# The stages before layer 0's scores, rearranged: adaLN loads, context tiles, weight products, PSUM pairs

## The chip, the cores and the metric

The kernel runs on one core of one Trainium2 chip. The metric is the device time of one execution in microseconds (us). The core has five engines that run beside each other and wait for one another through semaphores: TensorE (PE in the profile; its weight loads are PEld), VectorE (DVE), ScalarE (ACT), GpSimd (POOL) and SyncE (SP), which here issues most of the DMA transfers.

## What is computed

Two layers of a diffusion backbone over 1024 latent tokens and 256 context tokens, width 1024. Layer 0 mixes tokens by multi-head latent attention (16 heads), layer 1 by differential attention (8 heads). Cut to what matters for this change, which lies in layer 0:

```python
shift, scale, gate = split(silu(c) @ ada_w + ada_b, 3)           # latent; shift_c, scale_c, gate_c from c_ctx
h, h_c = x * (1 + scale) + shift, ctx * (1 + scale_c) + shift_c
q_lat, kv_lat, k_pe, g = split(h @ w_in, [256, 384, 416])        # the same for h_c
q = rms_norm(q_lat, g_qa) @ w_qb        # 16 heads of 64 + 32 (rotary)
k, v = split(rms_norm(kv_lat, g_kva) @ w_kvb)                    # 16 heads of 64 and 64; k_pe shared
o = softmax(q @ concat(k, k_c) * scale) @ concat(v, v_c)         # context queries see the context alone
x = layer_norm(ALPHA * x + gate * ((o * silu(g)) @ out_w)) 
```

## The kernel before, in words

The kernel keeps fp32 accuracy by splitting operands into a high part and a remainder (`split`, L175: ScalarE copies the high part, VectorE or GpSimd subtracts it) and multiplying three times (`mm3`, L184). Contraction over the width is in 8 blocks of 128 (`KT`); tokens are in 10 tiles of 128, of which 8 and 9 are context.

**Order of the work.** The program is written as straight Python; a scheduler orders the instructions of each engine and inserts the waits. Inside a `manual_schedule` block the engines named there (TensorE from L205 on, TensorE and VectorE in L880) keep the order in which the program is written; the other engines get theirs from the scheduler. SP issues its transfers in one in-order queue.

**adaLN (L196 to L251).** Per block `k` two 512 KB blocks of `ada_w` are loaded into six shared buffers (one of which holds a bias row first): for `g = 1` (the scale) TensorE multiplies the block by the broadcast SiLU of the conditioning (L228), for `g = 0` (the shift) VectorE accumulates it into `acc[0]` (latent) and `acc[1]` (context) (L232). From `k = 2` on, `in_weight(k - 2)` follows (L214): it loads 128 rows of the input weight's first 416 columns (208 KB) into a staging buffer `xt` (14 of them) and splits it into `wAH`, `wAL`; GpSimd subtracts for k = 6 and 7, VectorE otherwise. `shift_cols(s)` (L238) sums `acc[s]` over partitions on TensorE (L241) and copies the result to `cols0` (L243).

**Modulation and the latent projections (L254 to L385).** `h_part` loads a block of transposed tokens into an `xt` buffer and makes its modulated high part on ScalarE (L260) and its remainder on VectorE (L261, L263; for every third block GpSimd does L263). First all eight blocks of the context (both its tiles at once), then a few warm-up matmuls (L269), then `lat_mm` of tile 8 for blocks 0 to 3, then `shift_cols(0)`, then the first 512 latent tokens, then the rest of tile 8. The loop from L357 takes the other tiles in the order 9, 0 to 7, each with its eight blocks in one go; RMS statistics, normalisation, and turning (`lat_post`) follow three tiles behind.

**Gates and up-projection weights (L311 to L610).** TensorE works through 40 gate tiles (4 column groups of 10 token tiles). Beside them `up_weights` loads the Q and K weights: each block is multiplied by its norm gain on VectorE (L397 for Q, 768 columns; L307 for K and V, 512 columns) and split; squares of the weights (L407 to L410, ScalarE) are summed by TensorE (L418) to bound the values. Then `ada_dve` accumulates three more adaLN thirds on VectorE; the first product of each is L509, the others L511. `v_weight` loads the V weights.

**K, Q and V (L613 to L883).** PSUM has 8 banks of 512 columns. `set_banks` gives three pairs (tag `a`) and two single banks (`d`). A fixed list (L881) interleaves the generators: `pq`, `pk` project Q and K of head 0 and split them with a scale (`split16`), `vg` makes one V tile (L642 to L657), and `pm` makes the row of maxima for head 0: one step for each of four query tiles (L757, L759), one for the context's keys (L763 to L765), one that turns the row by TensorE (L768) and writes it into the Q operand (L769). For an even V tile ScalarE makes two copies and GpSimd the remainder (L650, L653, L654); for an odd one ScalarE makes one and VectorE the remainder (L650, L656).

**Heads (L905 to L957).** `run_step` takes units of scores, exponentials (L777), their casts (L778) and remainders (L779), with side work between. In head 0 the side work holds `ab1_of` and `h1_range` (L537 to L565): small VectorE instructions with one TensorE step (L552) that bound layer 1's input. They stand ahead of that head's `max0` in the program.

Of the kernel before, what the change touches and what calls it, by code (L numbers as in the profile page):

```python
# [53 lines left out]
def hybrid_kernel(  # L54
# [159 lines left out]
    def in_weight(k):  # L214
        ws = hs.tile([P, 512], F32, tag="xt", bufs=14, name=nm("ws"))
        sp.dma_start(ws[:, :NA], w_in[k * P:(k + 1) * P, :NA])
        split(wAH[:, k, :], wAL[:, k, :], ws[:, :NA], e_lo=pool if k > 5 else None)

    for k in range(KT):
        for g in (1, 0):  # L220
            w = hs.tile([P, D], F32, tag="adaw", bufs=6, name=nm("adaw"))
            sp.dma_start(w, ada_w[0, k * P:(k + 1) * P, g * D:(g + 1) * D])
            if k == 0 and g == 0:
                for s in range(2):
                    sp.dma_start(acc[s][0:1, :], ada_b[0:1, :D])
            if g:
                for j in range(KT):
                    pe.matmul(cbs[j // 4][:, j % 4, :], w[:, j * P:(j + 1) * P], scb[:, k, :], start=False,  # L228
                              stop=(k == KT - 1), skip_group_check=True)
            else:  # L230
                for s in (1, 0):
                    dve.scalar_tensor_tensor(acc[s], w, sc[:, 2 * k + s:2 * k + s + 1], acc[s], op0=ALU.mult, op1=ALU.add)  # L232
        if k > 1:
            in_weight(k - 2)
    for i in range(2):
        dve.tensor_scalar_add(cols0[:, 8 + 4 * i:12 + 4 * i, :], cbs[i][:, :, 0:2], 1.0)

    def shift_cols(s):  # L238
        cb = bank("d")
# [8 lines left out]
            mm3(ps[:, :NA], hH[:, k, ts], hL[:, k, ts], wAH[:, k, :], wAL[:, k, :], k == 0, k == KT - 1)  # L248

    shift_cols(1)  # L250
    for k in (6, 7):  # L251
        in_weight(k)

    def h_part(pool_, bufs, c0, n, k):  # L254

# [7 lines left out]
        (pool if k % 3 == 2 else dve).tensor_tensor(hL[:, k, c0:c0 + n], xt[:, :n], fv(hi), op=ALU.subtract)  # L263

    for k in range(KT):
        h_part(hs, 14, *CHUNKS[2], k)
    ps8 = bank("a")
    for _ in range(4):
        pe.matmul(ps8[:, :NA], idr, wAH[:, 0, :], start=True, stop=True)  # L269
    lat_mm(ps8, 8, range(4))  # L270
    shift_cols(0)
    for k in range(KT):
        h_part(hs, 14, *CHUNKS[0], k)
    lat_mm(ps8, 8, range(4, KT))
    hs_ctx.close()
    upw = rp.enter_context(spool("upw", side="right"))
    wqH = upw.tile([P, 2, 1536], F32R, name="wqH")
# [26 lines left out]

    def kv_weight(c, hi, lo, ws, e_lo=pool):
        sp.dma_start(ws, w_kv[:, c])
        dve.tensor_scalar_mul(ws, ws, gkva)  # L307
        split(hi, lo, ws, e_lo=e_lo)


# [30 lines left out]
    with spool("p0a") as pa:  # L341
# [15 lines left out]
        for t in (8, 9, 0, 1, 2, 3, 4, 5, 6, 7, None, None, None):  # L357
# [3 lines left out]
            if t is None:  # L361
# [1 line left out]
                    pass  # L363
                gate_tile(0, *wg)
                continue
            ps = ps8
            if t != 8:
                ps = bank("a" if t % 2 == 0 else "b")
                lat_mm(ps, t, range(KT))
            with tc.high_priority():  # L370
# [16 lines left out]
    def up_weights(pa):  # L387
# [5 lines left out]
        def q_weight(j, hh):  # L393
            c = slice(hh * 768, hh * 768 + 768)
            ws = u()
            sp.dma_start(ws, w_qb[j * P:(j + 1) * P, c])
            dve.tensor_scalar_mul(ws, ws, gqa[:, j:j + 1])  # L397
            split(wqH[:, j, c], wqL[:, j, c], ws)

        def k_weight(hh):  # L400
# [78 lines left out]
    def ada_dve(tile_, thirds):  # L479
# [25 lines left out]
        def add(k, s):  # L505
            ck = sc[:, 2 * k + s:2 * k + s + 1]
            if k == 0:
                acc.append(tile_("acc"))
                dve.tensor_scalar_mul(acc[s], ws[k], ck)  # L509
            else:  # L510
                dve.scalar_tensor_tensor(acc[s], ws[k], ck, acc[s], op0=ALU.mult, op1=ALU.add)  # L511

# [97 lines left out]
            pass  # L610
    p0.close()

    set_banks(a=3, d=2)  # L613
    a0 = ctx.enter_context(ExitStack())
    wk = a0.enter_context(spool("a0work"))
    Vh = wk.tile([P, NT, H0, V0 + 1], F16, name="Vh")
# [23 lines left out]
    def prod_v0():  # L640
        pool.memset(Vh[:, :, :, V0:V0 + 1], 1.0)
        for t in range(NT):  # L642
            ts = slice(t * P, (t + 1) * P)
            ps = pair()
            for hh in range(2):
                c = slice(hh * 512, hh * 512 + 512)
                mm3(ps[:, c], latH[:, 2, ts], latL[:, 2, ts], wv[0][:, c], wv[1][:, c], True, True)
            src = ps.rearrange("p (h d) -> p h d", d=V0)
            vh = Vh[:, t, :, :V0]
            act.activation(vh, src, AF.Copy, scale=vsc0)  # L650
            if t % 2 == 0:
                vf = w0("op").rearrange("p a b -> p (a b)")[:, :1024].rearrange("p (h d) -> p h d", d=V0)
                act.activation(vf, src, AF.Copy, scale=vsc0)  # L653
                pool.tensor_tensor(Vl[:, t, :, :], vf, vh, op=ALU.subtract)  # L654
            else:
                dve.scalar_tensor_tensor(Vl[:, t, :, :], src, vsc0, vh, op0=ALU.mult, op1=ALU.subtract)  # L656
            yield  # L657
# [221 lines left out]
    pm = max0(0, 0)  # L879
    with tc.manual_schedule(engines={ET.PE, ET.DVE}):  # L880
        for g in (pq, pk, pq, vg, pq, pq, vg, pk, pk, pq, pq1, vg, pq2, pq2, pq2, vg,  # L881
                  pm, vg, pm, vg, pm, vg, pm, vg, pm, vg, pm, vg):
            next(g)  # L883
    ow_ctx = ExitStack()

    def first(g, n):
# [18 lines left out]
    for h in range(H0):  # L905
# [42 lines left out]
        else:  # L948
            kq = chain(prod_k(h + 1), prod_q(h + 1, 0))
            low = [[(first(lw, 3), p_)] if h == H0 - 2 else [] for p_ in ((1, 0, 1, 0, 1), (1, 0, 1, 0, 1))]  # L950
            if h == 0:
                ab1_of()
            hr = [(h1_range(pair), (0, 1, 0, 1, 1))] if h == 0 else []
            run_step(units0(h, 0), hr + [(max0(h, 1), (1, 1, 2, 1, 1)), (max0(h, 2), (0, 1, 0, 1)),
                                    (kq, (2, 2, 1 + quad, 0, 0) if even else (2,))] + low[0])
            qs = chain(prod_q(h + 1, 1), prod_q(h + 1, 2))
# [719 lines left out]
```

## Time and profile before

| | us |
|---|---|
| median of 3 runs (lowest, highest) | 1806.28 (1804.34, 1807.49) |
| the profiled execution's own time | 1809.26 |
| its span, first to last instruction | 1807.5 |
| TensorE busy | 1671.3 |
| VectorE busy | 1241.4 |
| ScalarE busy | 1119.5 |
| GpSimd busy | 796.1 |
| mean granted TensorE clock (1 is full speed) | 0.986 |

The profile is one execution, and times in it count from its first instruction. A group's row gives line, engine, operation, output<-inputs and count, then busy time, the mean of one in ns, and the idle time ahead with what ended it. A wait's row gives who waited for whom, the total, the times and the longest. A row of the timeline gives start, duration, and in brackets the idle time before it. A row of the table of stretches gives each engine's busy time, the granted clock and the DMA engines' busy share and rate.

### The profile page before, as it was taken

Reading aid. Unit: us, or ns where it says so; the run is one execution under the profiler, and the core shown is the slowest. Engines: PE = TensorE matmul, PEld = TensorE weight load, DVE = VectorE, ACT = ScalarE, POOL = GpSimd, SP = SyncE. Lnnn points to the kernel's source line nnn. Section 1 sums busy time; section 2 is a strip of 40 time slices with the busy share of each in tenths; the row PEclk is TensorE's granted clock in tenths of the full one; section 3 lists DMA queues with packets and bytes.
Section 4 is the critical chain, followed back from the end, with each engine's and each line's share of the span. In section 5 each row is a group of like instructions: output and inputs, shape, how many; then the busy total and the mean of one; then the engine's idle time right before and its main releaser. Section 6 shows DMA issues by size and latency. Waiting matters only on the chain. (4 is left out here: it accounts for less than half of the span.)

```text
span 1807.5 us, 36761 instructions
## 1 busy us (share of the span) xinstructions
PE 1671.3 (92%) x14564; PEld 1236.1 (68%) x14564; DVE 1241.4 (69%) x2047; ACT 1119.5 (62%) x2233; POOL 796.1 (44%) x722
## 2 busy tenths in 40 slices
PE   7999979999999998999999999989999999986998
PEld 6999955656666665577766666767676757574776
DVE  7558575565665657547745777777877787969564
ACT  3541167777777787845535676767676766766442
POOL 1522146767776676835541222232314132435454
PEclk9999999999999999999999999999999999998999
DMA  8258510111111113164432213131212121223332
GB/s 303 80 157 263 160 46 22 42 45 25 37 44 36 46 39 103 33 212 160 144 108 59 80 54 78 54 80 54 68 41 58 40 66 55 67 61 121 97 120 70
DMA packets 111225, 154.84 MB, mean 86 GB/s; under 512 B 13415, under 2 KB 84679, under 8 KB 111054
## 3 DMA queue, kind: packets, MB, share of 16 engines
q1 hardware_dynamic: 102654, 144.90, 27.1%
q10 hardware_dynamic: 8400, 7.61, 1.3%
q8 instruction: 114, 1.87, 0.5%
q14 instruction: 57, 0.47, 0.1%
HBM read 98.65 MB, written 27.07 MB: 70 GB/s over the span
## 5 line engine op out<-in xcount | busy, mean ns | idle before, releaser
L779 POOL TENSOR_TENSOR pl<-p,ph 128x1024 f16<-128x1024 f32 (+1 forms) x176 | 366.1, 2085 | 153.6 <-ACT ph L778 127.0
L1358 ACT ACTIVATE p<-ps_b,mx 128x512 f32<-128x512 f32 (+1 forms) x384 | 230.7, 618 | 89.3 <-DVE mx L1354 85.2
L777 ACT ACTIVATE p<-ps_a,esc 128x1024 f32<-128x1024 f32 (+1 forms) x176 | 189.2, 1075 | 98.1 <-PE ps_a L835 92.1
L759 DVE TENSOR_REDUCE mx<-ps_a 128x1 f32<-128x1024 f32 x128 | 155.3, 1222 | 130.6 <-PE ps_a L757 130.6
L778 ACT CAST ph<-p 128x1024 f16<-128x1024 f32 (+1 forms) x176 | 177.1, 1006 | 5.5
L1352 DVE TENSOR_REDUCE mx<-ps_b 128x1 f32<-128x512 f32 x256 | 165.7, 682 | 0.0
L848 PE MATMUL ps_d<-Vh,pl 128*128 128x65 f16 x1344 | 147.1, 194 | 3.1 <-POOL pl L779 3.1
L845 PE MATMUL ps_d<-Vh,ph 128*128 128x65 f16 x1344 | 149.2, 196 | 0.0
L847 PE MATMUL ps_d<-Vl,ph 128*128 128x64 f16 x1344 | 148.0, 193 | 0.0
L1335 PE MATMUL ps_b<-KS,QS 128*128 128x512 f16 (+1 forms) x384 | 125.8, 345 | 13.8 <-DVE pl L182 7.2
L1383 POOL TENSOR_TENSOR sm<-sm,us 128x1 f32<-128x1 f32 x64 | 16.8, 262 | 273.3 <-DVE sm L1362 268.5
L845 PEld LDWEIGHTS <-ph 128*128 128x128 f16 x1344 | 123.9, 98 | 18.1 <-issue 5.0
L847 PEld LDWEIGHTS <-ph 128*128 128x128 f16 x1344 | 124.6, 99 | 12.4 <-issue 0.6
L833 PE MATMUL ps_a<-qH,KH 100*128 100x512 f16 x320 | 122.7, 383 | 10.0 <-ACT p L777 5.1
L1336 PE MATMUL ps_b<-KS,Q 128*128 128x512 f16 (+1 forms) x384 | 128.9, 345 | 0.0
L181 ACT ACTIVATE ph<-ps_b,lcf 128x512 f16<-128x512 f32 (+1 forms) x192 | 115.4, 649 | 19.1 <-PE ps_b L1371 19.1
L848 PEld LDWEIGHTS <-pl 128*128 128x128 f16 x1344 | 123.8, 98 | 4.3 <-POOL pl L779 4.2
L182 DVE SCALAR_TENSOR_TENSOR pl<-ps_b,lcf,ph 128x512 f16<-128x512 f32 (+1 forms) x192 | 117.2, 655 | 13.4 <-ACT ph L181 13.4
L1371 PE MATMUL ps_b<-idr,p 128*128 128x128 f32 x640 | 103.4, 278 | 22.7 <-ACT p L1358 14.8
L834 PE MATMUL ps_a<-qH,KL 96*128 96x512 f16 x320 | 122.5, 383 | 0.0
L835 PE MATMUL ps_a<-qL,KH 96*128 96x512 f16 x320 | 121.5, 380 | 0.0
L1381 PE MATMUL ps_b<-vh,pl 128*128 128x128 f16 x640 | 111.3, 220 | 5.3 <-DVE pl L182 5.3
(427 smaller groups left out, 5261.2 us busy)
## 6 DMA issues: line engine op xcount, KB each, us to landing
ws<-in_dw SPq DMA_DIRECT2D x28, 512.0 KB, 3.9
adw<-in_ada_w SPq DMA_DIRECT2D x24, 512.0 KB, 4.8
adaw<-in_ada_w SPq DMA_DIRECT2D x16, 512.0 KB, 7.5
g<-sg_d SPq DMA_DIRECT2D x16, 512.0 KB, 4.0
sg_d<-gg ACTq DMA_DIRECT2D x40, 128.0 KB, 3.4
o_d<-op SPq DMA_DIRECT2D x7, 640.0 KB, 3.9
xt<-in_xT SPq DMA_DIRECT2D x16, 256.0 KB, 4.4
wgs<-in_w_in SPq DMA_DIRECT2D x32, 128.0 KB, 2.7
```

The source lines that it names most:

```text
L759: dve.tensor_reduce(mx[:, t, 0:1], ps, axis=AX.X, op=ALU.max)
L777: act.activation(p32[:, :n], st, AF.Exp, scale=esc0)
L778: act.copy(ph[:, :n], p32[:, :n])
L779: pool.tensor_tensor(pl[:, :n], p32[:, :n], ph[:, :n], op=ALU.subtract)
L833: pe.matmul(s_, kh[:nr, ks], QH[:nr, :], start=True, stop=False)
L845: pe.matmul(pv[:, t, :], ph[:, ts], Vh[:, k, h, :], start=(k == kcs[0] and t == 0), stop=False, skip_group_check=True)
L847: pe.matmul(pv[:, t, :V0], ph[:, ts], Vl[:, k, h, :], start=False, stop=False, skip_group_check=True)
L848: pe.matmul(pv[:, t, :], pl[:, ts], Vh[:, k, h, :], start=False, stop=(k == NT - 1), skip_group_check=True)
L1335: pe.matmul(out, qs[m][:, ts], ks[m][:, c0:c0 + n], start=True, stop=False)
L1336: pe.matmul(out, q1[m][:, ts], ks[m][:, c0:c0 + n], start=False, stop=True)
L1352: dve.tensor_reduce(mx[:, 2 + 2 * m + i:3 + 2 * m + i], b, axis=AX.X, op=ALU.max, negate=True)
L1358: act.activation(p[m][:, c0:c0 + n], b, AF.Exp, bias=nb, accum_out=sm[:, 2 + 3 * m + i:3 + 3 * m + i])
```

## The change

In the order of the program:

- The input weights' blocks no longer stand among the adaLN blocks: `in_weight(k)` is called just before the context's `h_part` of the same block. GpSimd subtracts for every odd k. The last adaLN pair comes in the order shift, scale. The copies of the scale (L236) come after `shift_cols(1)`.
- Both context tiles have a PSUM bank from the start and are accumulated block by block, tile 8 and tile 9 in turn; `shift_cols(0)` comes after block 3 of both; the first 512 latent tokens come after all of it.
- The multiplications by norm gains (L307, L397) and the first product of each adaLN third (L509) go from VectorE to ScalarE.
- K, Q and V have four PSUM pairs and no single bank; the three pairs and two banks come back after the list. Odd V tiles now have their remainder from GpSimd, even ones from VectorE. In the list the context's maxima come ahead of V tiles 7 and 8, and the turned row ahead of the last.
- `ab1_of` and `h1_range` go from head 0 to head 2.

```diff
     def in_weight(k):
...
-        split(wAH[:, k, :], wAL[:, k, :], ws[:, :NA], e_lo=pool if k > 5 else None)
+        split(wAH[:, k, :], wAL[:, k, :], ws[:, :NA], e_lo=pool if k % 2 else None)
 
     for k in range(KT):
-        for g in (1, 0):
+        for g in (1, 0) if k < KT - 1 else (0, 1):
...
-        if k > 1:
-            in_weight(k - 2)
-    for i in range(2):
-        dve.tensor_scalar_add(cols0[:, 8 + 4 * i:12 + 4 * i, :], cbs[i][:, :, 0:2], 1.0)
...
     shift_cols(1)
-    for k in (6, 7):
-        in_weight(k)
+    for i in range(2):
+        dve.tensor_scalar_add(cols0[:, 8 + 4 * i:12 + 4 * i, :], cbs[i][:, :, 0:2], 1.0)
...
     for k in range(KT):
+        in_weight(k)
         h_part(hs, 14, *CHUNKS[2], k)
-    ps8 = bank("a")
+    psc = {8: bank("a"), 9: bank("b")}
     for _ in range(4):
-        pe.matmul(ps8[:, :NA], idr, wAH[:, 0, :], start=True, stop=True)
-    lat_mm(ps8, 8, range(4))
-    shift_cols(0)
+        pe.matmul(psc[8][:, :NA], idr, wAH[:, 0, :], start=True, stop=True)
+    for k in range(KT):
+        for t in (8, 9):
+            lat_mm(psc[t], t, (k,))
+        if k == 3:
+            shift_cols(0)
     for k in range(KT):
         h_part(hs, 14, *CHUNKS[0], k)
-    lat_mm(ps8, 8, range(4, KT))
...
     def kv_weight(c, hi, lo, ws, e_lo=pool):
-        dve.tensor_scalar_mul(ws, ws, gkva)
+        act.activation(ws, ws, AF.Copy, scale=gkva)
...
-            ps = ps8
-            if t != 8:
+            if t > 7:
+                ps = psc[t]
+            else:
...
-            dve.tensor_scalar_mul(ws, ws, gqa[:, j:j + 1])
+            act.activation(ws, ws, AF.Copy, scale=gqa[:, j:j + 1])
...
-                dve.tensor_scalar_mul(acc[s], ws[k], ck)
+                act.activation(acc[s], ws[k], AF.Copy, scale=ck)
...
-    set_banks(a=3, d=2)
+    set_banks(a=4)
...
-            if t % 2 == 0:
+            if t % 2:
...
         for g in (pq, pk, pq, vg, pq, pq, vg, pk, pk, pq, pq1, vg, pq2, pq2, pq2, vg,
-                  pm, vg, pm, vg, pm, vg, pm, vg, pm, vg, pm, vg):
+                  pm, vg, pm, vg, pm, vg, pm, pm, vg, vg, pm, vg):
             next(g)
+    set_banks(a=3, d=2)
...
-            if h == 0:
+            if h == 2:
                 ab1_of()
-            hr = [(h1_range(pair), (0, 1, 0, 1, 1))] if h == 0 else []
+            hr = [(h1_range(pair), (0, 1, 0, 1, 1))] if h == 2 else []
```

## The prediction

> **What bounds the kernel now.** I read the page first, for the shares, then the table of stretches, since the change touches only what comes before layer 0's scores (to 256 us) and one step in each of heads 0 and 2.
>
> ```profile
> span 1807.5 us, 36761 instructions
> PE 1671.3 (92%) x14564; PEld 1236.1 (68%) x14564; DVE 1241.4 (69%) x2047; ACT 1119.5 (62%) x2233; POOL 796.1 (44%) x722
> ```
> ```profile
> core 0: us, PE busy (x) PEld busy (x) DVE busy (x) ACT busy (x) POOL busy (x), PEclk, DMA share, GB/s
> 4.00:31.00 27.00, 20.71 (x143) 19.54 (x144) 20.39 (x21) 2.79 (x6) 0.76 (x1) 1.00 1.01 381
> 42.00:108.00 66.00, 66.00 (x428) 64.84 (x426) 38.06 (x70) 36.76 (x112) 28.31 (x40) 1.00 0.42 122
> 108.00:118.00 10.00, 7.61 (x57) 6.74 (x55) 8.26 (x17) 4.18 (x9) 0.00 (x0) 1.00 0.41 117
> 118.00:221.00 103.00, 102.97 (x828) 98.91 (x828) 73.36 (x93) 22.87 (x56) 21.91 (x24) 1.00 0.66 195
> 221.00:256.00 35.00, 27.52 (x119) 19.64 (x118) 23.24 (x22) 21.27 (x24) 12.21 (x7) 0.96 0.31 81
> 251.00:257.00 6.00, 3.90 (x11) 2.32 (x12) 2.66 (x4) 3.14 (x3) 2.06 (x1) 0.72 0.00 0
> 273.00:278.00 5.00, 5.00 (x38) 2.75 (x36) 1.23 (x1) 2.16 (x2) 1.60 (x2) 0.66 0.01 3
> ```
>
> TensorE is busy 92% of the span, and where it is full (42 to 108, 118 to 221) no other engine's saving shows: there only what TensorE itself starts earlier counts, and it counts whole, because everything behind follows TensorE. The rest divides in four: the adaLN stage, where the DMA engines are full (share 1.01, 381 GB/s) and TensorE waits; 2.4 us of waits in 108 to 118; 7.5 us of waits in 221 to 256 (K, Q, V), with the granted clock at 0.72 at their end; and head 0, where the clock is again at 0.66. The four terms of the sum are these four places.
>
> **Term 1: adaLN first, context block by block.** First the transfer rate, then steps in order of time, then the weight loads' group (count, busy, mean ns).
>
> ```profile
> 16.00:28.00 12.00, 7.55 (x62) 6.88 (x60) 10.18 (x12) 1.76 (x4) 0.00 (x0) 1.00 1.02 397
> ```
> ```profile
> 19.69 0.42 SPq L216 DMA_DIRECT2D ws<-in_w_in  x1
> 21.05 2.14 SPq L222 DMA_DIRECT2D adaw<-in_ada_w  x2
> ...
> 30.65 2.48 DVE L232 SCALAR_TENSOR_TENSOR hacc<-adaw,sc,hacc 128x1024 f32<-128x1024 f32 x2
> 31.99 2.05 PE L241 MATMUL ps_d<-ones,hacc 128*128 128x128 f32 x16 [0.72 <-DVE hacc L232]
> 34.69 4.05 ACT L260 ACTIVATE hH<-xt,cols 128x256 fp32r<-128x256 f32 x8 [1.87 <-DVE cols L243]
> 38.93 1.95 PE L241 MATMUL ps_d<-ones,hacc 128*128 128x128 f32 x16
> 41.12 5.76 ACT L260 ACTIVATE hH<-xt,cols 128x512 fp32r<-128x512 f32 x8 [2.37 <-DVE cols L243]
> 50.12 1.28 DVE L263 TENSOR_TENSOR hL<-xt,hH 128x512 fp32r<-128x512 f32 x2
> ```
> ```profile
> L187 PEld LDWEIGHTS ps_b<-wAH,hL 128*128 128x128 f32 x28 | 5.2, 188 | 0.1
> ```
>
> SP's queue goes in program order; the in_weight transfer at 19.69 is the fifth, so five of them (128x416 fp32, 0.213 MB) stand ahead of the last adaLN block. Without them it lands 5 x 0.213 MB / 397 GB/s = 2.7 us sooner. Now the context can start 4.0 us after the last block (30.65 to 34.69: 1.3 of VectorE, the 2.05 of L241, copies). With the last pair turned round, the last block feeds TensorE instead: sixteen matmuls of the same size (2.05) and then L241's (2.05), 4.25 with a copy. The first context tile therefore starts 2.7 - 0.25 = 2.4 us sooner, at 32.3.
>
> That is not what reaches TensorE's end. The shift of the latent tokens (L241 at 38.93) stands behind four blocks of one token tile now, of two tiles then. Full, TensorE gives a matmul of 416 columns per weight load, 0.19 us, so four blocks of two tiles take 4 x 6 x 0.19 = 4.6 us, plus 0.6 for the first activation (4.05 / 8) and its hand-over, against the 4.24 from 34.69 to 38.93 now. Its end, and the start of the latent tiles behind it, comes at 32.3 + 5.2 + 2.0 + 0.1 = 39.6 instead of 41.1: 1.5 sooner. Behind it VectorE needs some 9.4 us for the eight blocks (from near 42 to 51.40, where the row at 50.12 ends), and tile 0's last matmul can only follow; the second context tile (4.5 us) now fills the time before it. So tile 0 ends some **1.4 us** sooner and everything behind follows. The moved transfers are 24 issues of 0.33 to 0.42 us; context tile 7 must wait for a freed staging buffer (16 tiles, 14 buffers) until about 33, and lands well before its block is due at 39. Ends of the range: -2.4, if the order of the shift costs nothing; +1.7 below.
>
> ```profile
> L177 POOL TENSOR_TENSOR wAL<-ws,wAH 128x416 fp32r<-128x416 f32 x2 | 3.1, 1558 | 27.6 <-ACT wAH L176 27.6
> 268.63 1.76 DVE L556 TENSOR_TENSOR hm<-hm 128x1 f32<-128x1 f32 x1
> ```
>
> Two more of the weights' remainders go to GpSimd, 1.56 us each, and they now lie beside VectorE's work on the context. A VectorE subtraction of one element took 1.76 us while GpSimd worked, so these can hold VectorE: at worst 2 x 1.56 = 3.1, which makes term 1 +1.7. The Trainium skill, "SBUF — State Buffer", section "Who interferes with whom", says that such a VectorE instruction and a GpSimd one take turns at one port pair, the second blocked until the first is done. By that rule taken whole the sum below would be -4.0; the trace agrees for L556, but VectorE finished other context tiles beside GpSimd.
>
> **Term 2: ScalarE multiplies the weights.**
>
> ```profile
> L397 DVE TENSOR_SCALAR u<-u,gqa 128x768 f32<-128x768 f32 x4 | 2.5, 617 | 4.7 <-DMA u<-in_w_qb 4.7
> L176 ACT CAST wqH<-u 128x768 fp32r<-128x768 f32 x4 | 3.3, 832 | 2.2 <-DVE u L397 2.2
> L407 ACT ACTIVATE wsq<-u,gkva 128x512 fp32r<-128x512 f32 x2 | 1.4, 724 | 1.3 <-DMA u<-in_w_kv 1.3
> PE ps_c L418 <- DVE u L294: 1.3, 1, 1.3
> PE ps_c L418 <- ACT wsq L407: 1.1, 1, 1.1
> ```
>
> ScalarE's multiply at 768 elements is not in the trace: the cast of that size is 0.83, and a scaled activation at 512 takes 0.72. Scaled to 768 that is at most 1.09; I take 0.94. Multiply and cast now stand on one engine, 1.77 us a block, where VectorE's 0.62 and 0.95 set 1.57. What is queued behind: the later casts, the gate tiles' SiLU, and L407, for which TensorE already waits 1.1 us. The second block's buffer, in which L407's operand arrives, is freed about 0.9 us later, so I take **+0.9**. Ends: -1.3 (VectorE loses 2.5 us and more of work, and the second wait goes) and +3.5 (six products of some 0.6 us show). The six products of L509 and the two of the V weights lie in 118 to 221, where ScalarE is busy 22.87 of 103: TensorE's 102.97 covers them, at nothing; without that cover each would cost a microsecond.
>
> **Term 3: four pairs for K, Q and V.**
>
> ```profile
> PE ps_a L768 <- DVE ng L765: 2.1, 1, 2.1
> PE ps_a L185 <- DVE stqL L182: 2.0, 1, 2.0
> PE ps_a L757 <- DVE Vl L656: 1.4, 2, 0.7
> PE ps_a L185 <- DVE mx L759: 1.1, 2, 0.5
> PE ps_a L185 <- DVE Vl L656: 0.8, 1, 0.8
> L656 DVE SCALAR_TENSOR_TENSOR Vl<-ps_a,vsc,Vh 128x1024 f16<-128x1024 f32 x4 | 5.1, 1282 | 4.7 <-ACT Vh L650 4.7
> L295 DVE TENSOR_TENSOR rr<-rr,rsw 128x1024 f32<-128x1024 f32 x1 | 3.1, 3052 | 0.0
> L653 ACT ACTIVATE op<-ps_a,vsc 128x1024 f32<-128x1024 f32 x5 | 5.5, 1108 | 0.0
> ```
>
> All of TensorE's waits, 7.4 us, are for VectorE to give a PSUM pair back (four rows) or for the row of maxima (L768). Six microseconds at 0.72 behind that wait lose 6 x 0.28 = 1.7 more. So 9.1 could go. VectorE bounds what goes: its work here is 23.24 us plus one more remainder of 1.28, minus 1.8 if L295 comes down to the 1.28 of as many elements in L656 once tile 0's remainder is off GpSimd, so 22.7 from 223.6, when the first operand is there: 246.3. TensorE without waits would end at about 247. With a fourth pair each wait for a pair moves one pair back, and two V tiles stand between the context's maxima and the row: 12 matmuls at 512/416 x 0.19 = 0.23, 2.8 us. VectorE has a V remainder, two maxima (1.2 each) and their joining before the row, 3.9 us, so that 1.3 stay at L768 with the hand-overs; 0.5 at the first score (the row's last step), and 0.6 for the pairs elsewhere, by going through the order by hand. So 9.1 - 2.4 = -6.7. The last V tile goes from VectorE to ScalarE, which has a second 1.11 us copy ahead of the first exponential (2.2 for both, while TensorE makes the scores in 1.3): +0.9. Term 3 is **-5.8**. Ends: -8.2 (no wait left), -2.9 (only the row's wait and the clock go).
>
> **Term 4: the layer-1 range moves from head 0 to head 2.**
>
> ```profile
> PE ps_a L768 <- DVE hm L300: 1.4, 1, 1.4
> PE ps_a L833 <- DVE qH L769: 1.4, 1, 1.4
> 334.68 2.13 POOL L779 TENSOR_TENSOR pl<-p,ph 128x1024 f16<-128x1024 f32 x1 [0.76 <-ACT ph L778]
> ```
>
> In head 0 the chain of small VectorE instructions stands ahead of the row of maxima and TensorE waits twice, 2.8 us, and then runs five microseconds at 0.66, 1.7 more: 4.5 goes. In head 2 the program order is the same, and a GpSimd subtraction runs at the same point (334.68), so the same chain has the same 2.8 to pay, and perhaps the clock: I take +3.7. Net **-0.8**, ends -4.5 and +0.5.
>
> **The sum.** -1.4 + 0.9 - 5.8 - 0.8 = -7.1 us. The profiled execution took 1809.26 (1.8 around its span), so 1802.2 there; the median of the runs shown is 1806.28, 3.0 lower, so **1799.2**.
>
> **Rivals.** (a) Larger gain: the chain finds VectorE idle in head 2 (term 4 -4.5), the shift's order costs nothing (term 1 -2.4), and the first exponential isn't held (term 3 -6.7): with term 2, -12.7, **1793.6**. For it: VectorE has gaps in the steady heads. Against: program order is unchanged. (b) Little gain, since VectorE, not the pairs, binds: term 1 +1.7, term 3 -2.9, with +0.9 and 0: -0.3, **1806.0**. For it: GpSimd's hold on VectorE, and VectorE's 23.24 of 35; against: the pairs' rows name it. This is also where a schedule that changes less than the text does would end. (c) Slower: waiting block by block for context, TensorE falls to half clock there. The 48 matmuls and the shift's sixteen then cost twice, 9.1 + 2.05 = +11.2: +4.1, **1810.4**. It decides where TensorE is idle about as much as in 251 to 257 (3.90 of 6). Against it: in 4 to 31 it was busy 20.71 of 27, with gaps, at 1.00. The Trainium skill, "TensorE: Matmul & The Clock Gate", Part 1, asks an idle window of about 3.4 us before the clock halves, so by it (c) can't come; here the clock fell after a wait of 2.1 us, so the measurement keeps (c) open.
>
> **How the numbers follow.** Forecast 0.56, (a) 0.24, (b) 0.14, (c) 0.06. Between runs about 0.2% (3.6 us) can be told from no change, so faster means below 1802.7: the forecast, (a) and the best of (b), 0.82; within 0.2%: 0.12; slower: 0.06. The range reaches past (a) to the terms' better ends and into (b): 1791.5 to 1805.
>
> **What would show it.** Term 1: the first context activation near 32.3, tile 0's last matmul near 50.5, six microseconds of context work beside GpSimd without long VectorE instructions. Term 2: L418's waits at 3.3 in sum instead of 2.4. Term 3: the row L768 waiting 1.3, waits in the stretch at 2.4, clock above 0.95 there, L295 near 1.2. Term 4: no wait on the range's chain in head 0, one of 2.8 in head 2. The prediction is wrong if VectorE still has its pairs waited for, or if L418 waits over 6 us.

## The result and the profile after

| | before | after |
|---|---|---|
| median of 7 runs each, side by side (lowest, highest), us | 1807.02 (1803.48, 1809.51) | 1811.38 (1810.38, 1815.61) |
| ratio of the times, 95% interval | | 1.0031 (1.0018 to 1.0044) |
| the profiled execution | 1809.26 | 1810.68 |

The change made the kernel slower by 5.6 us (3.3 to 8.0), where 7.1 us less were forecast. First the page of the changed kernel, the rows of the whole span.

```profile
span 1808.8 us, 36762 instructions
PE 1673.5 (93%) x14564; PEld 1239.2 (69%) x14564; DVE 1228.4 (68%) x2031; ACT 1130.7 (63%) x2247; POOL 794.0 (44%) x724
```

The totals say almost nothing: ScalarE has 11 us more, VectorE 13 less. The table of stretches of the changed kernel (columns as before the change) says where to look. The K, Q and V stage now lies at 228 to 258.

```profile
4.00:31.00 27.00, 22.32 (x154) 21.34 (x155) 20.29 (x18) 1.60 (x4) 1.54 (x2) 1.00 0.99 365
42.00:108.00 66.00, 61.01 (x377) 57.31 (x376) 30.05 (x62) 35.54 (x109) 28.07 (x40) 1.00 0.35 103
108.00:118.00 10.00, 6.61 (x48) 6.31 (x47) 5.94 (x9) 8.88 (x15) 0.00 (x0) 0.84 0.62 196
118.00:221.00 103.00, 102.36 (x820) 99.44 (x820) 71.43 (x93) 31.52 (x66) 20.23 (x22) 0.98 0.61 186
228.00:258.00 30.00, 26.91 (x124) 19.73 (x123) 22.10 (x23) 20.19 (x22) 10.37 (x6) 1.00 0.39 103
```

TensorE was full from 42 to 108 (66.00 of 66); it now stands idle there for 5 us. From 108 to 118 the clock is 0.84 instead of 1. The K, Q and V stage has 3.1 us of waits instead of 7.5, and the clock stays up. The waits of TensorE in the changed kernel, the first two over the whole span, the others from 221 to 262:

```profile
PE ps_a L187 <- DVE hL L259: 3.6, 4, 2.4
PE ps_c L418 <- ACT wsq L407: 3.4, 1, 3.4
...
PE ps_a L768 <- DVE ng L765: 0.9, 1, 0.9
PE ps_a L185 <- DVE Vl L656: 0.9, 3, 0.4
PE ps_a L185 <- ACT op L653: 0.9, 1, 0.9
PE ps_a L833 <- DVE qH L769: 0.7, 1, 0.7
PE ps_a L757 <- DVE stpL L182: 0.4, 1, 0.4
```

The two first rows are the new waits: mostly for the latent tokens' blocks (L187; 2.8 of the 3.6 lie from 72 to 76), and for the squares of the V weights (L418, 1.1 us before). Where the two executions stand apart, at marks that both have (us, start in the trace):

| mark | before | after | later by |
|---|---|---|---|
| first context matmul (L185) | 35.34 | 33.19 | -2.16 |
| tile 0 done (first transpose) | 52.07 | 52.85 | +0.78 |
| first gate tile | 87.40 | 91.62 | +4.21 |
| first column sum (L418) | 109.70 | 116.24 | +6.54 |
| first Q matmul (gates done) | 220.64 | 228.50 | +7.86 |
| first exponential, head 0 | 257.70 | 260.24 | +2.54 |
| head 1 | 290.04 | 287.23 | -2.81 |
| head 3 | 351.63 | 353.67 | +2.04 |
| last exponential of layer 0 | 769.93 | 769.26 | -0.67 |
| TensorE's last matmul ends | 1798.98 | 1800.37 | +1.39 |

So by place: the first term +4.2, the second +3.7, the third -5.3, the fourth -5.35 and +4.85. The sum is +2.0 at head 3. The last 2.7 us of layer 0 are not of the change: in head 14 of the kernel before TensorE waited 2.27 us, and the clock was halved behind it in that one execution (first fence, before; second, after).

```profile
718.00:724.00 6.00, 6.00 (x36) 2.93 (x35) 3.85 (x8) 4.21 (x5) 3.36 (x3) 0.50 0.67 197
```
```profile
720.00:726.00 6.00, 5.04 (x68) 3.23 (x66) 5.52 (x8) 5.47 (x6) 4.62 (x3) 1.00 0.65 198
```

Head 14 takes 33.5 us there, 30.9 after and 30.1 to 32.4 in the eighteen experiments. Without it the two profiled executions would differ by some 4.1 us instead of 1.4, near the 4.4 of the medians. Single executions of the kernel before lie between 1800.9 and 1810.9, so below a few us the marks of a stage say more than the whole time. Layer 1 adds 2.1 us in small steps, which is scatter of the same kind (823.5 us from its first exponential to TensorE's last matmul before, 825.6 after, 822.5 to 825.6 in the experiments).

### The profile page after: what moved, and what is told of

The parts are those of the page before. It is cut to its first block, busy times and chain, and to the rows that moved or that the text cites. A ratio compares the mean times of both kernels' runs of the same rounds, so it can differ in the third digit from the quotient of the medians.

```text
span 1808.8 us, 36762 instructions
## 1 busy us (share of the span) xinstructions
PE 1673.5 (93%) x14564; PEld 1239.2 (69%) x14564; DVE 1228.4 (68%) x2031; ACT 1130.7 (63%) x2247; POOL 794.0 (44%) x724
```

## The experiments

Each ratio is to the kernel before, run beside it on the same chip. My theory after the two traces (A): the parts act each by itself, and the first group alone loses, since the second half of the latent tokens comes late. The rival (B): the groups cost only together.

**The four groups one by one.** Each is the kernel before with that term's hunks of the diff above, which begin with these lines:

```diff
# t1_alone: in_weight, the adaLN loop, cols0, psc and the loop of lat_mm
+        split(wAH[:, k, :], wAL[:, k, :], ws[:, :NA], e_lo=pool if k % 2 else None)
# t2_alone: L307, L397, L509
+        act.activation(ws, ws, AF.Copy, scale=gkva)
# t3_alone: set_banks, the parity of the V tiles, the list
+    set_banks(a=4)
# t4_alone: ab1_of, h1_range
+            if h == 2:
```

> The kernel before with the first group of edits alone (adaLN blocks ahead of the input weights, context block by block). Theory A: this group is what loses, by itself, because the blocks of the second half of the latent tokens pass through three staging buffers and VectorE's order puts other work ahead of the first of them; TensorE then waits about 2.8 us in the middle of the projections (near 72 to 76). Then the gates start 4 us later than in the kernel before and the time is 3 to 5 us longer. Theory B: the loss comes of the groups together, the context's order alone gives the 1.4 us that were predicted: the gates start 1 to 2 us sooner, the time is 1 to 2 us shorter.

> The kernel before with the multiplications on ScalarE alone. Theory A: ScalarE's queue holds the squares of the K and V weights behind the K weights' multiplications and casts; the wait of TensorE for them grows from 1.1 to about 3.4 us, and with the other delays the time is 2.5 to 3.7 us longer. Theory B: the squares are late only because the first group moved everything in front of them; alone, the multiplications cost 1 us or less.

> The kernel before with four PSUM pairs for K, Q and V alone. Theory A: the stretch from the first V tile to the first exponential is 5.3 us shorter as in the changed kernel, and the time falls by 4.5 to 6 us. Theory B: part of the gain was that TensorE came later into this stretch and found more work done ahead; alone it gives 3 us or less.

> The kernel before with the range of layer 1's input moved from head 0 to head 2 alone. Theory A: head 0 is 5 us shorter and head 2 is 5 us longer, the time is within 1.5 us of the kernel before. Theory B: head 0 in the kernel before waits behind the row of maxima in any case, the move gives back less than it takes, and the time is 2 us or more longer.

| kernel | median us | ratio (interval) | by the ratio, us |
|---|---|---|---|
| t1_alone | 1813.06 | 1.0043 (1.0027 to 1.0058) | +7.8 |
| t2_alone | 1809.25 | 1.0015 (1.0003 to 1.0027) | +2.7 |
| t3_alone | 1802.16 | 0.9980 (0.9969 to 0.9991) | -3.6 |
| t4_alone | 1807.10 | 1.0003 (0.9995 to 1.0012) | +0.5 |

The sum, +7.4, agrees with the +5.6 (3.3 to 8.0) of all together. At the marks A holds in all four: t1_alone had the gates 5.93 us later, t2_alone the first Q matmul 3.76 later, t3_alone brought 5.43 us between the first Q matmul and the first exponential, t4_alone -4.8 in head 0 and +4.8 in head 2. By the times, the first group lost even more than A said, and t3_alone's -3.6 lies between A (4.5 to 6) and B (3 or less). The profiles of all kernels offer a reason: the stretch from the first Q matmul to the first exponential took 31.6 to 32.0 us in the eleven with four pairs, but 35.4 to 37.8 in the nine with three. In these nine TensorE waits 2.1 us at L768, and in only four of them, the kernel before among them, the clock is halved behind it. The average gain is 4.8 us, within t3_alone's interval.

**Where the first group loses.** Its two halves, one by one: the loads with the remainders on GpSimd (`t1_ada`), and the context tiles' order (`t1_ctx`).

```diff
# t1_ada: in_weight, adaLN and cols0 as in the change; the context as before
-        split(..., e_lo=pool if k > 5 else None)
+        split(..., e_lo=pool if k % 2 else None)
...
     for k in range(KT):
+        in_weight(k)
         h_part(hs, 14, *CHUNKS[2], k)
# t1_ctx: psc and the block-by-block loop as in the change; loads as before
```

> The kernel before with the loads' half of the first group alone: adaLN blocks ahead of the input weights, last pair turned round, every second remainder on GpSimd; the context's tiles are multiplied as before (tile 8 in two halves round the shift, then tile 9). Theory A: the loss of the first group lies in the context's order, which lets ScalarE and VectorE put tile 0's statistics and normalisation ahead of the first block of the second half of the latent tokens; here the old order stays, the earlier adaLN counts, and the time is 1 to 2.4 us shorter than before. Theory B: the loss lies in the moved weights (remainders on GpSimd beside VectorE, staging buffers): the time is 2 us or more longer.

> The kernel before with the other half of the first group alone: both context tiles block by block, the shift of the latent tokens behind four blocks of both, the first latent tokens behind all of it; loads as before. Theory A: the loss is here: TensorE waits 2.4 us or more near 74 to 78 for the late blocks, and tile 0 ends 2 to 3 us later; the time is 5 to 8.5 us longer than before. Theory B: it needs both halves; alone this one costs 2 us or less.

t1_ctx is at 1.0041 (1.0027 to 1.0055), +7.4 us, as A says: the context's order alone loses what the group loses. Tile 0 ended only 1.46 us later, less than A's 2 to 3; the rest is a wait of 2.27 us for a late block at 73, with the clock at 0.53 from 76 to 79. t1_ada is at 1.0006 (0.9994 to 1.0017): the loss isn't there, but neither is the 1 to 2.4 us of gain that A expected. Why the order matters is in ScalarE's and VectorE's queues. The timelines, first of the kernel before, then of the changed one.

```profile
52.37 0.82 ACT L260 ACTIVATE hH<-xt,cols 128x512 fp32r<-128x512 f32 x1
...
53.09 0.37 ACT L373 ACTIVATE junk<-ps_a 128x256 f32<-128x256 f32 x1
...
53.80 0.69 DVE L263 TENSOR_TENSOR hL<-xt,hH 128x512 fp32r<-128x512 f32 x1
...
54.52 3.17 SPq L258 DMA_DIRECT2D xt<-in_xT  x2
...
70.71 0.69 DVE L263 TENSOR_TENSOR hL<-xt,hH 128x512 fp32r<-128x512 f32 x1
...
71.94 0.35 PE L187 MATMUL ps_a<-wAH,hL 128*128 128x416 f32 x1
```
```profile
52.81 0.38 ACT L373 ACTIVATE junk<-ps_a 128x256 f32<-128x256 f32 x1 [3.43 <-PE ps_a L187]
...
54.19 0.83 ACT L256 ACTIVATE hH<-xt,cols 128x512 fp32r<-128x512 f32 x1
...
54.78 0.48 DVE L378 TENSOR_SCALAR ln<-ps_a,rs 128x256 f32<-128x256 f32 x1 [0.77 <-POOL rs L160]
...
56.95 1.29 DVE L259 TENSOR_TENSOR hL<-xt,hH 128x512 fp32r<-128x512 f32 x2
...
57.75 4.97 SPq L254 DMA_DIRECT2D xt<-in_xT  x3
...
75.30 0.69 DVE L259 TENSOR_TENSOR hL<-xt,hH 128x512 fp32r<-128x512 f32 x1
```

Before, ScalarE makes the first block of the second half (L260, 52.37) ahead of tile 0's squares (L373). In the changed kernel those squares come first: ScalarE waits 3.43 us for tile 0, and the block's product starts at 54.19, and VectorE has tile 0's normalisation (54.78) ahead of the first remainder (56.95 instead of 53.80). (ScalarE stands idle as long before, 3.62 us, but for tile 8's normalisation.) Why the scheduler turned the order round was not tested. There are three staging buffers, so the fourth load goes out at 57.75 instead of 54.52, and so on down the chain to the last block, 75.30 instead of 70.71. The last row of the first fence is what the prediction should have looked at: tile 4's last matmul took that block at 71.94, and the block was ready at 70.71 + 0.69 = 71.40. TensorE was full, but with half a microsecond to spare. All twenty kernels agree with this reading. Counted from tile 0's end (its mark), TensorE wants the last block after 19.9 us (71.94 - 52.07), and it is ready after:

| ScalarE's order, staging buffers | kernels | us |
|---|---|---|
| block first, three | before, t2_alone, t3_alone, t4_alone, t1_ada, t2_q, t3_late, t23_late, t3_sqin, t23_sqin | 19.0 to 19.4 |
| squares first, three | ada_v; t1_ctx, t1_alone, after | 22.0; 22.9 to 23.1 |
| squares first, four | bufs4, cured, cured_v, fix_v, ada_v4, best | 18.0 to 18.4 |

Only the four kernels of the second row wait there. No run puts the old order alone back into the changed kernel. The remedy is another buffer (`bufs4`, on the changed kernel):

```diff
-                    h_part(pa, 3, *CHUNKS[1], k)
+                    h_part(pa, 4, *CHUNKS[1], k)
-                ln = pa.tile([P, NA], F32, tag="ln", bufs=4, name=nm("ln"))
+                ln = pa.tile([P, NA], F32, tag="ln", bufs=3, name=nm("ln"))
-            kpt = pa.tile([ROPE, P], F32, tag="kpt", bufs=2, name=nm("kpt"))
+            kpt = pa.tile([ROPE, P], F32, tag="kpt", bufs=1, name=nm("kpt"))
```

> The changed kernel with four staging buffers in place of three for the second half of the latent tokens (room made by three buffers for the normalised rows in place of four, and one for the rotary keys in place of two). Theory A: the wait of 2.44 us at 72.4 is a chain through the three buffers (a block's load waits until an earlier block's remainder is done); with a fourth each load is issued a block sooner and the wait of 2.8 us goes for the most part: 1808.5 to 1809.5 us. Rival: the order of the engines sets it, the blocks stand behind the normalisation of a tile whichever buffer they have: within 1 us of the changed kernel's 1811.4.

1807.90, 1.0014 (1.0005 to 1.0022): by the ratios 3.1 us below the changed kernel, a little more than A's 1.9 to 2.9. From tile 0's end to the first gate it takes 0.1 us longer than before, where the changed kernel took 3.4 longer; the waits for VectorE's blocks that are left (the row of bufs4) lie in the context and in tile 0.

```profile
PE ps_a L187 <- DVE hL L259: 0.9, 2, 0.5
```

**VectorE beside GpSimd.** In the changed kernel tile 0 is done 2.9 us later after the first context matmul than before. The timeline of the changed kernel there:

```profile
35.70 0.58 DVE L177 TENSOR_TENSOR wAL<-ws,wAH 128x416 fp32r<-128x416 f32 x1
...
36.06 1.16 POOL L177 TENSOR_TENSOR wAL<-ws,wAH 128x416 fp32r<-128x416 f32 x1 [0.43 <-ACT wAH L176]
...
36.20 1.31 DVE L259 TENSOR_TENSOR hL<-xt,hH 128x256 fp32r<-128x256 f32 x1
...
37.86 0.43 DVE L259 TENSOR_TENSOR hL<-xt,hH 128x256 fp32r<-128x256 f32 x1
...
38.24 1.95 PEld L237 LDWEIGHTS ps_d<-ones,hacc 128*128 128x128 f32 x16
...
39.66 1.12 POOL L177 TENSOR_TENSOR wAL<-ws,wAH 128x416 fp32r<-128x416 f32 x1
...
39.88 1.18 DVE L259 TENSOR_TENSOR hL<-xt,hH 128x256 fp32r<-128x256 f32 x1
...
41.76 0.16 DVE L239 COPY cols<-ps_d 128x8 f32<-128x8 f32 x1
...
41.95 0.82 ACT L256 ACTIVATE hH<-xt,cols 128x512 fp32r<-128x512 f32 x1 [3.60 <-DVE cols L239]
```

The same subtraction takes 0.43, or 1.31 and 1.18 where a GpSimd remainder runs beside it (36.06 to 37.22, 39.66 to 40.78). The copy of the latent shift (41.76, 0.85 later than before) stands behind them in VectorE's queue; before, it came right behind its matmuls (L241 ends at 40.88, the copy starts at 40.91). Here the last weights for its matmuls (L237) had been loaded at 38.24 + 1.95 = 40.19, and ScalarE waited 3.60 us for the copy (L256). Two kernels test it, both with a second edit meant as a remedy for the second term, the squares asked for later:

```diff
# cured: bufs4, and
-                     + sq[:2] + rc + sq[2:]
+                     + rc + sq
# cured_v: cured, and
-        split(..., e_lo=pool if k % 2 else None)
+        split(..., e_lo=None)
```

> The changed kernel with both causes taken out that the runs so far name: four staging buffers for the second half of the latent tokens, and the squares behind the rotary chunks. Theory A: the two are the whole of what went wrong but for VectorE's longer context work (2 to 3 us up to tile 0's end): 3.1 us for the buffers and 4 to 6 us for the sums below the changed kernel, 1802 to 1804.5 us, 1 to 4 us below the kernel before. Rival: the first group has further losses behind it: 1806 us or more.

> As cured, with all eight remainders of the input weights on VectorE, none on GpSimd. Theory A: in the changed kernel two of VectorE's remainders of the context (0.43 us by themselves) took 1.31 and 1.18 us, each until a GpSimd remainder beside it had ended; without those VectorE loses the holds and gets two products of 0.58 us more in that stretch: the row of shifts is copied near the same time or up to 1 us sooner, all its rows at 0.41 to 0.58, and the time is within 1.5 us of cured. Rival: the long rows are not GpSimd's doing: rows of 1.2 us stay, the copy comes 1.2 us or more later, and the time is 1 to 2 us longer than cured's.

cured came to 1810.30, 1.0023 (1.0013 to 1.0034): a miss: the later list is no remedy (below). In its profiled execution the clock was also at 0.50 from 28 to 34. cured_v is at 1809.66, 1.0019 (1.0008 to 1.0031), within 1.5 us of it. In cured the two rows of 1.31 and 1.18 are there, from VectorE's first product for the context to the copy 8.60 us; in cured_v all such rows are at 0.41 to 0.43 and it is 7.70, with two more remainders of 0.58 in it. So the holds are GpSimd's doing. From the first context matmul to tile 0's end (us):

| context order, remainders | kernels | us |
|---|---|---|
| as before, beside adaLN | before and the eight others with the first group's code as before | 16.7 |
| as before, beside the context, VectorE | ada_v, ada_v4, best | 17.6 each |
| as before, beside the context, half on GpSimd | t1_ada | 18.9 |
| block by block, beside adaLN | t1_ctx | 18.3 |
| block by block, beside the context, VectorE | cured_v, fix_v | 18.8, 18.8 |
| block by block, beside the context, half on GpSimd | t1_alone, after, bufs4, cured | 19.7, 19.7, 19.8, 20.0 |

Weights' remainders moved beside the context: 0.9. Half of them on GpSimd: 0.9 to 1.3 more. The context block by block, with the shift behind two tiles: 0.8 to 1.6 more.

**Does the earlier adaLN bring anything?** `ada_v` is t1_ada with all remainders on VectorE, `ada_v4` that with the fourth buffer.

```diff
# ada_v
-        split(..., e_lo=pool if k % 2 else None)
+        split(..., e_lo=None)
# ada_v4: that, and the three lines of bufs4
```

> The kernel before with adaLN blocks ahead of the input weights, the context's tiles as before, and all remainders of the input weights on VectorE. Theory A: without GpSimd's holds VectorE is through the context 0.9 us sooner than with every second remainder on GpSimd, and the time is 0.5 to 1.5 us below that version's, at the kernel before within 1 us; the earlier adaLN brings nothing because VectorE does the same remainders later, beside the context. Rival: the earlier adaLN counts as predicted: 1.4 to 2.4 us below the kernel before.

> As ada_v, with four staging buffers for the second half of the latent tokens (three for the normalised rows, one for the rotary keys). In ada_v tile 0 ended 0.5 us sooner than in the kernel before, and TensorE then waited 1.8 us for the second half's blocks. Theory A: what comes sooner at tile 0 is kept only if the second half's blocks come sooner too; with the fourth buffer that wait goes and the gates start 0.3 to 1.5 us sooner than in the kernel before, the time is 1 to 2.5 us below ada_v's. Rival: the blocks are late for another reason: the wait stays over 1 us, the time is ada_v's.

ada_v: 1807.88, 1.0014 (1.0004 to 1.0024), not below t1_ada. Its first context matmul was 1.42 us sooner than before, tile 0 0.50 sooner, and then TensorE waited 1.41 and 0.36 us for the second half's blocks. The order had turned round here too, though the context's tiles are as before; rows of ada_v:

```profile
51.88 0.39 ACT L370 ACTIVATE junk<-ps_a 128x256 f32<-128x256 f32 x1
...
52.83 0.82 ACT L256 ACTIVATE hH<-xt,cols 128x512 fp32r<-128x512 f32 x1
...
55.10 0.48 DVE L375 TENSOR_SCALAR ln<-ps_a,rs 128x256 f32<-128x256 f32 x1 [0.86 <-POOL rs L160]
...
55.76 0.68 DVE L259 TENSOR_TENSOR hL<-xt,hH 128x512 fp32r<-128x512 f32 x1
```

Tile 0's squares and normalisation stand ahead of the first block's product and remainder, and the fourth load goes out at 56.46 instead of 54.52. So a gain of 0.50 became a loss of 1.82 at the first gate. ada_v4: 1806.65, 1.0006 (0.9996 to 1.0015); that wait is gone, as A says, but the gates start 1.1 us later than before, not sooner, because the start wasn't sooner in that execution. Rows of the kernels ada_v and ada_v4, TensorE's last adaLN product, and t1_ada's clock there:

```profile
29.20 2.05 PE L228 MATMUL ps_c<-scb,adaw 128*128 128x128 f32 x16 [2.37 <-DMA adaw<-in_ada_w]
```
```profile
28.83 3.54 PE L228 MATMUL ps_c<-scb,adaw 128*128 128x128 f32 x16 [1.98 <-DMA adaw<-in_ada_w]
```
```profile
30.00:32.00 2.00, 2.00 (x11) 2.00 (x11) 2.00 (x3) 1.08 (x2) 1.01 (x1) 0.50 0.93 295
```

In nine of the ten kernels with adaLN first TensorE waits 1.8 to 2.5 us for the last block (1.13 before), and in five of the ten (in two of the ten others) the clock was halved at the last adaLN products, which costs up to 1.7 us of the 2.4 (in ada_v4 above 3.54 us instead of 2.05, in cured 3.78). In these ten the first context matmul came between 2.2 us sooner and 1.4 later than before. The stream is also slower: in 16 to 28 the kernels with adaLN first moved 346 to 386 GB/s, the ten others 391 to 401.

**What ScalarE's multiplications cost.** In `t2_q` only the four products of the Q weights go to ScalarE.

> The kernel before with only the four products of the Q weights by their gain on ScalarE; those of the K and V weights and of the adaLN thirds stay on VectorE. Theory A: ScalarE's queue alone sets when the squares of the V weights come; two products of 0.72 us less stand ahead of them than with all moved, so TensorE waits 2.0 to 2.5 us instead of 3.5, its clock stays up or nearly so, and the time is 0.5 to 1.7 us longer than before. Rival: the loads are late because their buffers come free late; the wait stays at 3.3 us or more, with half the clock behind it, and the time is 2.5 us or more longer.

```diff
             sp.dma_start(ws, w_qb[j * P:(j + 1) * P, c])
-            dve.tensor_scalar_mul(ws, ws, gqa[:, j:j + 1])
+            act.activation(ws, ws, AF.Copy, scale=gqa[:, j:j + 1])
```

1806.61, 1.0007 (0.9997 to 1.0016): TensorE's first wait is 1.66 us, less than either theory said, and its clock stays up; the time is A's. The table of stretches of t2_alone, with all products on ScalarE:

```profile
108.00:112.00 4.00, 0.64 (x6) 0.43 (x4) 2.85 (x4) 3.97 (x8) 0.00 (x0) 0.84 0.54 162
112.00:117.00 5.00, 4.88 (x22) 4.79 (x23) 4.31 (x10) 0.79 (x2) 0.00 (x0) 0.50 0.29 88
```

ScalarE is busy 3.97 of 4 us while TensorE has 0.64; then TensorE runs five microseconds at half clock. To tell ScalarE's queue from late loads, two kernels ask for the sums later (`t3_late`, the kernel before with the third term; `t23_late`, with the second and third), and two load the squares' operand into buffers of its own (`t3_sqin`, `t23_sqin`):

```diff
# t3_late, t23_late
-                     + sq[:2] + rc + sq[2:]
+                     + rc + sq
# t3_sqin, t23_sqin
-            wv = u(512)
+            wv = pa.tile([P, 512], F32, tag="wsv", bufs=2, name=nm("wsv"))
-            sq = u(512).bitcast(F32R) if i else pa.tile([P, 512], F32R, tag="wsq", ...)
+            sq = u(512).bitcast(F32R)
```

> The kernel before with the four PSUM pairs alone, and the first two squares of the V weights behind the rotary chunks in the list of the weights' jobs, so that TensorE asks for their sums three gate tiles (about 9 us) later. If the two waits at the sums (1.06 and 1.33 us in the kernel before) come only of asking too early, they go and the time is 2 us or more below that of the four pairs alone, 5.5 to 7 us below the kernel before. Rival: the wait goes to the next of the sums or to the rotary chunks: as the four pairs alone, about 4 us below.

> As t3_late, with the multiplications on ScalarE too (all eleven of the change). Theory A: what they cost is the wait at the sums of squares and the half clock behind it, and nothing else: with the sums asked for later their cost goes, and the time is within 1.5 us of t3_late's. Rival: ScalarE's queue costs in other places as well (gate tiles, later weights): 2.5 us or more above t3_late.

> The kernel before with the four PSUM pairs, and the loads of the V weights for the squares in two buffers of their own (the squares go to the shared ones), so that they don't wait for a shared buffer; all multiplications on VectorE. If the load's buffer sets TensorE's first wait at the sums (1.06 us in the kernel before), it falls below 0.5 us and the time is 1 to 2 us below the four pairs alone (5 to 6 us below the kernel before). Rival: the squares stand behind the casts of the weights on ScalarE: the wait stays near 1 us, the time is that of the four pairs alone.

> As t3_sqin with the multiplications on ScalarE. ScalarE's order still has the squares behind all eight Q and K products and casts. Theory A: that queue sets the wait; the earlier loads change little, the first wait is 2.3 us or more (3.5 us with the multiplications alone), and the time is 2 us or more above t3_sqin's. Rival: the loads' buffers set it: the wait falls below 1.2 us, and the time is within 1 us of t3_sqin's.

The later list was wrong in both: 0.9996 (0.9987 to 1.0006) and 1.0006 (0.9997 to 1.0015), so t3_late loses 3 us against t3_alone, and t23_late is 1.8 above t3_late, between A and its rival (the change moves fourteen products, not the eleven of that expectation). The loads of the squares now stood behind the rotary chunks, which use the same five buffers, and went out at 114.8 instead of 105.4; TensorE waited 4.14 us, then ran at 0.58. With buffers of their own the loads are early, and the two kernels differ (waits of t3_sqin from 100 to 130, then of t23_sqin):

```profile
PE ps_c L418 <- ACT u L409: 2.9, 1, 2.9
PE ps_c L418 <- ACT u L407: 0.3, 1, 0.3
```
```profile
PE ps_c L418 <- ACT u L407: 3.7, 1, 3.7
```

With the products on VectorE the first wait falls to 0.3 (and a later sum waits 2.9 instead, so nothing is won: 0.9993, 0.9984 to 1.0001, not below t3_alone's 0.9980). With them on ScalarE it stays at 3.7: the squares wait for ScalarE, not for their data. t23_sqin's ratio is 1.0002 (0.9991 to 1.0013), some 1.6 us above; A's 2 us is within what the intervals allow.

**The named causes together.** `fix_v` is the changed kernel with the fourth buffer, `e_lo=None` and the squares' own buffers; `best` is ada_v4 with the third term.

```diff
# fix_v: the changed kernel with the edits of bufs4, t3_sqin and
-        split(..., e_lo=pool if k % 2 else None)
+        split(..., e_lo=None)
# best: ada_v4 with those of t3_alone
```

> The changed kernel with four staging buffers for the second half of the latent tokens, all remainders of the input weights on VectorE, and the squares' loads in buffers of their own. Theory A: the buffers give 3.1 us, the remainders 0.6 to 1.2 us, the squares' loads 0 to 1 us: 1806 to 1808 us, within 2 us of the kernel before; what is left of the first group's and the multiplications' price (ScalarE's queue at the sums with half the clock behind it, 4 us) eats the gain of the four pairs. Rival: the loads were the cause at the sums as well: 1803 us or less.

> As ada_v4, with the four PSUM pairs: the parts that paid and the repaired first group, without the multiplications on ScalarE and without the move of the range. If the gains add, 1800 to 1802 us, as the four pairs alone (0.998 of the kernel before) or up to 1.5 us below. Rival: an earlier start is lost again before the K, Q and V stage (at the sums of squares): 1803 us or more.

fix_v: 1806.10, 1.0007 (0.9996 to 1.0017), 4.3 us below the changed kernel, as A says; what is left is ScalarE's queue (TensorE waits 3.20 us for the squares). best: 1802.94, 0.9979 (0.9969 to 0.9990), between the two expectations and the same as the four PSUM pairs alone (0.9980): the repaired first group adds nothing that these runs can tell. The version to keep is the kernel before with the third term alone.

## Why the prediction was wrong, step by step

**Term 1: predicted -1.4, at the marks +4.2, alone +7.8. This is the step that failed**, in the sentence "So tile 0 ends some 1.4 us sooner and everything behind follows". Its first half: tile 0 ended 0.78 us later. The start came 2.16 us sooner in the changed kernel (2.4 predicted), but often less, since the stream was slower (346 to 386 GB/s, not 397) and the wait for the last block can halve the clock. The shift behind two tiles was priced at 1.0 and took 0.8 to 1.6. Not priced: the weights' remainders themselves, moved from beside the adaLN loads, where VectorE waited for data, to the context, where it sets the pace (0.9). GpSimd's hold stood only in the bound of +1.7: it took 0.9 to 1.3. The Trainium skill, "SBUF — State Buffer", section "Who interferes with whom", has a VectorE instruction with two inputs in SBUF contend with a GpSimd one that reads SBUF; the trace agrees (0.43 alone, 1.31 and 1.18 beside GpSimd). The trace of the kernel before had such a row too, which the prediction didn't use: VectorE's remainder of the weights, 0.58 by itself, took 1.46 while GpSimd made its two (from 32.35 to 35.43).

```profile
33.05 1.46 DVE L177 TENSOR_TENSOR wAL<-ws,wAH 128x416 fp32r<-128x416 f32 x1
```

Its second half: "everything behind follows" took TensorE's full 66 us as the only bound, and left out the chain that feeds it through three buffers. With the order of the kernel before that chain does follow tile 0's end, 0.5 to 0.9 us ahead of TensorE, in ten of ten kernels; in the changed kernel tile 0's squares and normalisation stand ahead of its first block, the last block is ready 3.8 us later after tile 0's end, and 3.4 us are lost, which a fourth buffer takes away (bufs4).

**Term 2: predicted +0.9, +3.7 at the marks, alone +2.7; mis-sized, near its bound of 3.5.** The multiply took the 0.94 us that I chose. What was too small is the wait: 3.4 for the first sum, 4.0 with the second, instead of 3.3 for both; the squares come behind all six products (four of Q, two of K) and their casts, not one block's delay later. And the half clock behind a wait of 3.4 us was priced in terms 3 and 4 but not here.

**Term 3: predicted -5.8, -5.3 at the marks; right.** L768 waits 0.9 (1.3 predicted), 3.8 in the stretch and at the first score (2.4), the clock is at 1.00, L295's sum is down to 1.22 (1.2), and from the last V tile to the first exponential it takes 2.25 us instead of 1.76 (0.9 more predicted). By the median it is 3.6 (1.6 to 5.6), by the average of all profiles 4.8: the 1.7 us of half clock that the prediction counted on losing stood in the one execution that it read, and in four of nine in all. That the marks came so near to -5.8 is in part the luck of that execution.

**Term 4: predicted -0.8 from -4.5 and +3.7; -5.35 and +4.85, alone +0.5 (-0.9 to 2.2); right.** The chain pays in head 2 what it paid in head 0.

**Rivals.** (c), 1810.4, had the right sign and nearly the time, but by luck: TensorE didn't fall to half clock among the context's blocks, but behind the adaLN wait and at the sums. None named the second half of the latent tokens.

## What to carry to other kernels

A full engine does not show how little its supply has to spare: for each operand of a stage that is to start earlier, look up when it was ready and when it was used; here half a microsecond lay between. Work that was hidden beside a wait for loads costs its whole length when it is moved beside the engine that sets the pace, and an automatic order of the queues can change with the program's order, so look for what now stands ahead of the next load's consumer. Price half the clock as a risk behind every wait of two microseconds or more, and don't count its end as a sure gain: the same wait had it in one execution and not in another.

## What the runs showed of the hardware that was not expected

- The clock doesn't fall by the length of a wait alone. It was halved behind waits of 1.89 (cured_v), 1.98 (ada_v4), 2.27 (best), 2.43 (t1_alone, at 73), 2.45 (t1_ada) and 3.39 us (after), and not behind 1.85 (fix_v), 2.29 (bufs4), 2.37 (ada_v), 2.44 (after, at 72) and 2.89 us (t3_sqin, at 115). Behind the same wait of 2.11 to 2.12 us at L768 it was halved in before, t1_alone, t4_alone and t2_q, and not in t2_alone, t1_ada, t1_ctx, ada_v and ada_v4. The Trainium skill, "TensorE: Matmul & The Clock Gate", Part 1, asks an idle window of about 3.4 us; here less can do.
- The same DMA engines at a busy share of 0.97 to 1.01 moved 346 to 386 GB/s when the adaLN blocks came in one row through their six buffers, and 391 to 401, at 1.01 to 1.03, with the weights' transfers between them. Why was not tried.
